# Shifts and scales of the norms as row sums on the vector engine

## The chip, the cores and the metric

One core of a Trainium2 chip runs the whole kernel. The metric is the device time of one execution in microseconds. Engines: PE is the matrix engine, PEld its weight loads, DVE the vector engine, ACT the scalar engine, POOL the general engine, SP the engine that issues most transfers.

## The reference

A two-layer decoder trunk on 256 tokens of width 1024, all in float32. Before every sub-layer stands a norm whose shift and scale come from one conditioning vector `c`:

```python
c_act = jax.nn.silu(c)
mod = jnp.einsum('bd,dn->bn', c_act, w_ada[layer]) + b_ada[layer]
sh1, sc1, gt1, sh2, sc2, gt2 = [m[:, None, :] for m in jnp.split(mod, 6, axis=-1)]
h = rms_norm(x, g_attn[layer]) * (1.0 + sc1) + sh1
x = x + gt1 * hybrid_mixer(h, ...)
h = rms_norm(x, g_ffn[layer]) * (1.0 + sc2) + sh2
x = x + gt2 * (swiglu(h, ...) if layer == 0 else moe_swiglu(h, ...))
```

`w_ada` is 1024 x 6144 for each layer: a vector times a matrix, of which each layer needs six pieces of 1024 columns (shift, scale and gate, twice). Layer 0 ends in a dense feed-forward of width 2816, layer 1 in a mixture of eight experts.

## The kernel before, in words

The kernel runs in the order: first norm, first attention, second norm, dense feed-forward, third norm, second attention, fourth norm, experts, last norm. Activations have tokens or features on the 128 partitions as needed; every large weight is loaded by SP into a ring of three `raw` buffers and split by ACT (line 164) and DVE (line 168) into two parts, which PE multiplies three times (lines 186 to 188, 340, 870 to 872).

The shift and scale of a norm are made by `Mod` (line 213), in two halves of 512 features. `half(q)` is a generator: it clears an accumulator `ada` on POOL and loads the bias row into it (lines 195, 197), then takes eight blocks of `w_ada`, 128 input features x 1024 columns (512 of the shift, 512 of the scale), each loaded by SP into one of two `rada` buffers (line 209) and added on DVE with `c` as the scalar of a partition (line 211). The sum over partitions is left to PE: eight products with a column of ones (line 233, sixteen PE instructions) put the 1024 sums into PSUM, 128 of them to a column, and DVE takes them from there (lines 239, 240). `gate` (line 245) makes a gate with the same accumulation and a product with a matrix of ones (line 255).

These generators are strewn into other work: `filler(parts, steps)` (line 921) gives a function `fill` that at its i-th call advances the generators by `steps[i]`; a step is two blocks, and each half or gate has five steps, the last being the sum and its reading. In attention `fill` is called at set places of the code (after the projections, after each branch and token half, and once with 20 to finish, line 794), in the feed-forward twice for each of its blocks and once with 30 before the last block (line 905). The first norm's halves are made by `Start` with the same accumulators, ahead of all else. Both halves of the second norm and a gate are made in the first attention (lines 938 to 940), a gate, the third norm, a gate and the fourth norm in the feed-forward (line 949), and one gate in the second attention (line 986).

A scheduler puts the traced instructions of each engine in an order of its own: an instruction whose inputs are free can move ahead of ones traced before it. In the two attentions, and in the feed-forward, `after_split` and `issue_after` hold some DVE work behind a given instruction. Every engine then works its list in order, so a waiting instruction holds what is behind it.

Of the kernel before, what the change touches and what calls it, by code (L numbers as in the profile page):

```python
# [12 lines left out]
F32 = mybir.dt.float32  # L13
# [35 lines left out]

RAW, RAWX, W1B, W2B, ADAB, RADA = 3, 6, 3, 3, 2, 2  # L50
PARTS = [2]
# [4 lines left out]
def trunk(ctx: ExitStack, tc: tile.TileContext, x, c, positions, w_in, w_out, diff_lambda, diff_subln,  # L56
# [10 lines left out]
    def ps_a(name):  # L67
        return psum.tile([P, 512], F32, tag="a", name=name, bufs=4)
# [14 lines left out]
    def pre1(shape, dt, name):  # L83
        return pre.tile(shape, dt, name=name, bufs=1)
# [6 lines left out]
    nc.gpsimd.dma_start(posi, positions.rearrange("b (t p) -> (b t) p", p=P))  # L91
    vrows = pre1([48, P], F32, "vrows")
    nc.gpsimd.dma_start(vrows[0:16], g_attn.rearrange("l (k p) -> (l k) p", p=P))
    nc.gpsimd.dma_start(vrows[16:32], g_ffn.rearrange("l (k p) -> (l k) p", p=P))
    nc.gpsimd.dma_start(vrows[32:48], b_ada[0, 0:2 * D].rearrange("(k p) -> k p", p=P))

# [116 lines left out]
    class Mod:  # L213


        def __init__(self, l, which, g0, queue):
            self.l, self.base, self.g0, self.queue = l, which * 3072, g0, queue
            self.piece = 3 * which
# [3 lines left out]
        def columns(self, q):  # L222
            return [self.base + 512 * q, self.base + D + 512 * q]
# [37 lines left out]
    gT = pre1([P, 4 * KC], F32, "gT")  # L261
    m1 = Mod(0, 0, 0, nc.scalar)

# [145 lines left out]
    with tc.tile_pool(name="start", bufs=1, reuse_waits="tile") as sp, tc.issue_after(silu_c.ins), in_order():  # L409

        bT = sp.tile([P, 2, KC], F32, name="bT")

        class Start:


            def __init__(self, q):
                self.q = q
                self.acc = pre.tile([P, 1024], F32, tag="ada", name="ada", bufs=ADAB)

            def sums(self):  # L420
                q = self.q
                pc = ps_b("pc")
                T.matmul(pc[:, 0:8].rearrange("p (a k) -> p a k", a=2), ident, bT[:, :, 4 * q:4 * q + 4],
                         start=True, stop=False)
# [13 lines left out]
        for k in range(KC):  # L438
            first.block(k)
            if k in (1, 5):  # L440
                t = k // 5
                nc.sync.dma_start(xs[:, t], x[0, t * P:(t + 1) * P, :])
                for n in range(2):
                    nm0.part(t, n)
                nm0.finish(t, True)
            if k == 5:
                pv = ps_c("pv")
                T.transpose(pv[:, 0:48], vrows, ident[:48, :48])
                V.tensor_copy(gT, pv[:, 0:32])
                V.tensor_copy(bT.rearrange("p a k -> p (a k)"), pv[:, 32:48])  # L450
        vi = pj_i.split(0, 4)
# [20 lines left out]
        pj_a.unit(0, 4, va, terms=(2,))  # L472
    ada_raw[:] = [pre, RADA]


# [461 lines left out]

    m2 = Mod(0, 1, 16, nc.gpsimd)
    finish = attention(0, h, pj_i, pj_a, filler([m2.half(0), m2.half(1), gate(0, 0, "g1")],
                                                 (0, 1, 0, 0, 4, 0, 0, 3, 1, 4, 1, 1)), yp)  # L940
    with tc.tile_pool(name="ffn", bufs=1, reuse_waits="tile") as fp:
# [3 lines left out]
        for t in range(NT):  # L945
            ffn.first(h, t, st["units"])
        m1 = Mod(1, 0, 8, nc.gpsimd)
        m2 = Mod(1, 1, 24, nc.gpsimd)
        fill = filler([gate(0, 1, "g2"), m1.half(0), m1.half(1), gate(1, 0, "g1"), m2.half(0), m2.half(1)], (3, 0, 1, 0, 3, 0, 6, 0, 6, 0, 0, 0, 0, 4, 2, 1, 1))
        nm = Norm("a1")  # L950
# [540 lines left out]
def _laid_out(name, a):  # L1491
# [7 lines left out]
    if name == "w_ada":  # L1499
        a = a.reshape(DEPTH, KC, P, 2, 3, 1024)  # L1500
        shift, scale = (a[..., i, :].reshape(DEPTH, KC, P, 2, 2, 512) for i in range(2))
        mods = np.stack([shift, scale], 5).reshape(DEPTH, KC, P, 2, 2, 1024)
        a = np.concatenate([mods, a[..., 2:, :]], 4).reshape(DEPTH, KC, P, 6, 1024)
        return a.transpose(0, 3, 1, 2, 4)
    if name in ("w_ff_gate", "w_ff_up"):
# [27 lines left out]
```

## Time and profile before

| | us |
|---|---|
| median of three runs | 1309.76 |
| lowest, highest | 1303.88, 1314.73 |
| the profiled execution | 1308.91 |
| its span, first to last instruction | 1307.1 |
| PE busy | 1230.5 (94%) |
| DVE busy | 1091.4 (83%) |
| ACT busy | 832.9 (64%) |

Busy times overlap, and a PE that shows as busy need not be at its peak: a row of its timeline gives start, length and, in brackets, the idle time in front of it with what ended it. [...] Rows of one timeline may overlap a little, because the next instruction starts while the one before it drains.

### The profile page before, as it was taken

Reading aid. Unit: us, or ns where it says so; the run is one execution under the profiler, and the core shown is the slowest. Engines: PE = TensorE matmul, PEld = TensorE weight load, DVE = VectorE, ACT = ScalarE, POOL = GpSimd, SP = SyncE. Lnnn points to the kernel's source line nnn. Section 1 sums busy time; section 2 is a strip of 40 time slices with the busy share of each in tenths; the row PEclk is TensorE's granted clock in tenths of the full one; section 3 lists DMA queues with packets and bytes.
Section 4 is the critical chain, followed back from the end, with each engine's and each line's share of the span. In section 5 each row is a group of like instructions: output and inputs, shape, how many; then the busy total and the mean of one; then the engine's idle time right before and its main releaser. Section 6 shows DMA issues by size and latency. Waiting matters only on the chain.

```text
span 1307.1 us, 17866 instructions
## 1 busy us (share of the span) xinstructions
PE 1230.5 (94%) x6601; PEld 1036.0 (79%) x6601; DVE 1091.4 (83%) x1236; ACT 832.9 (64%) x1010; POOL 52.5 (4%) x88
## 2 busy tenths in 40 slices
PE   4989899999999899899999999999999999999996
PEld 4779779989887787677888877788878778788784
DVE  7898677787768864687899987899986999978996
ACT  3654563433446555457788856788855898667785
POOL 3101000010001000000000000000000000000001
PEclk9999899999989899889999999999999999999999
DMA  9557828988963433568999998899998999998991
GB/s 382 206 170 239 293 93 309 318 315 302 331 241 113 137 122 129 225 235 290 385 396 420 419 412 308 324 404 420 421 382 292 358 419 420 420 350 319 410 361 56
DMA packets 63679, 396.90 MB, mean 304 GB/s; under 512 B 7718, under 2 KB 8032, under 8 KB 23264
## 3 DMA queue, kind: packets, MB, share of 16 engines
q1 hardware_dynamic: 62928, 395.60, 79.4%
q8 instruction: 54, 0.88, 0.3%
q14 instruction: 41, 0.34, 0.1%
q0 software_dynamic: 640, 0.07, 0.0%
q10 hardware_dynamic: 16, 0.00, 0.0%
HBM read 394.60 MB, written 1.05 MB: 303 GB/s over the span
## 4 chain that ended last, share of the span: by engine, by line
PE 62%; DVE 10%; issue 8%; ACT 4%; POOL 0%; POOLq 0%; ACTq 0%; DVEq 0%
DVE w L168 6%; PE gu L187 5%; PE gu L186 5%; PE gu L188 5%; PE gu L1269 4%; PE gu L1268 4%; PE dn L186 4%; PE dn L188 4%; PE dn L187 4%; PE pj L340 3%; PE dn L1268 3%; PE dn L1269 2%; PE ptl L1284 2%; PE gu L870 2%; PE gu L872 2%
## 5 line engine op out<-in xcount | busy, mean ns | idle before, releaser
L164 ACT ACTIVATE w<-raw 128x1024 fp32r<-128x1024 f32 (+3 forms) x203 | 258.9, 1293 | 164.4 <-PE gu L871 37.2
L168 DVE TENSOR_TENSOR w<-raw,w 128x1024 fp32r<-128x1024 f32 (+3 forms) x203 | 303.8, 1512 | 50.8 <-ACT w L164 50.3
L168 DVE TENSOR_TENSOR w<-rawx,w 128x2048 fp32r<-128x2048 f32 (+1 forms) x134 | 300.2, 2252 | 26.5 <-ACT w L164 26.2
L164 ACT ACTIVATE w<-rawx 128x2048 fp32r<-128x2048 f32 (+1 forms) x134 | 252.2, 1887 | 16.4 <-PE gu L187 9.2
L340 PE MATMUL pj<-w,h 128*128 128x384 f32 (+3 forms) x672 | 134.0, 351 | 1.2 <-ACT h L182 0.5
L211 DVE SCALAR_TENSOR_TENSOR ada<-rada,cT,ada 128x1024 f32<-128x1024 f32 x80 | 102.3, 1279 | 32.7 <-DMA rada<-in_w_ada 32.6
L340 PEld LDWEIGHTS pj<-w,h 128*128 128x128 f32 x672 | 112.9, 192 | 11.4 <-ACT h L182 2.4
L168 DVE TENSOR_TENSOR w2x<-rawx,w1x 128x2048 fp32r<-128x2048 f32 (+1 forms) x45 | 100.6, 2237 | 12.9 <-ACT w1x L164 12.9
L186 PE MATMUL gu<-w,hh 128*128 128x512 f32 (+1 forms) x288 | 110.5, 384 | 0.0
L1269 PE MATMUL gu<-w,hh 128*128 128x512 f32 (+1 forms) x288 | 107.4, 380 | 3.2 <-DVE w L168 2.8
L187 PE MATMUL gu<-w,hh 128*128 128x512 f32 (+1 forms) x288 | 109.2, 379 | 0.0
L188 PE MATMUL gu<-w,hh 128*128 128x512 f32 (+1 forms) x288 | 109.1, 379 | 0.0
L1268 PE MATMUL gu<-w,hh 128*128 128x512 f32 (+1 forms) x288 | 106.7, 377 | 0.0
L870 PE MATMUL gu<-h,w 128*128 128x256 f32 x320 | 91.5, 286 | 0.0
L872 PE MATMUL gu<-h,w 128*128 128x256 f32 x320 | 90.6, 283 | 0.0
L871 PE MATMUL gu<-h,w 128*128 128x256 f32 x320 | 90.5, 283 | 0.0
L164 ACT ACTIVATE w1x<-rawx 128x2048 fp32r<-128x2048 f32 (+1 forms) x45 | 84.4, 1878 | 4.7 <-PE gu L187 2.5
L1269 PEld LDWEIGHTS gu<-w,hh 128*128 128x128 f32 x288 | 54.1, 188 | 18.8 <-DVE w L168 8.5
L188 PEld LDWEIGHTS gu<-w,hh 128*128 128x128 f32 x288 | 54.6, 190 | 10.8
L187 PEld LDWEIGHTS gu<-w,hh 128*128 128x128 f32 x288 | 54.8, 190 | 10.4 <-issue 0.5
L186 PEld LDWEIGHTS gu<-w,hh 128*128 128x128 f32 x288 | 54.6, 190 | 10.5 <-issue 0.5
L1268 PEld LDWEIGHTS gu<-w,hh 128*128 128x128 f32 x288 | 54.1, 188 | 10.4
(348 smaller groups left out, 2508.7 us busy)
## 6 DMA issues: line engine op xcount, KB each, us to landing
rawx<-in_w_exp_down SPq DMA_DIRECT2D x72, 1024.0 KB, 7.4
rawx<-in_w_exp_up SPq DMA_DIRECT2D x55, 1024.0 KB, 7.6
rawx<-in_w_exp_gate SPq DMA_DIRECT2D x49, 1024.0 KB, 8.3
rada<-in_w_ada SPq DMA_DIRECT2D x96, 512.0 KB, 5.2
raw<-in_w_exp_gate SPq DMA_DIRECT2D x39, 1024.0 KB, 8.0
raw<-in_w_exp_up SPq DMA_DIRECT2D x33, 1024.0 KB, 7.8
raw<-in_w_exp_down SPq DMA_DIRECT2D x16, 1024.0 KB, 7.3
raw<-in_w_ff_gate SPq DMA_DIRECT2D x11, 1024.0 KB, 7.1
```

Source lines behind the costliest of these rows:

```text
L164: last_split[0] = A.activation(v1[:, s], r[:, s], AF.Copy)
L168: last_split[1] = V.tensor_tensor(v2[:, s], r[:, s], v1[:, s].bitcast(F32), op=ALU.subtract)
L186: T.matmul(ps, l1, r1, start=start, stop=False)
L187: T.matmul(ps, l2, r1, start=False, stop=False)
L188: T.matmul(ps, l1, r2, start=False, stop=stop)
L211: V.scalar_tensor_tensor(acc, r, cT[:, k:k + 1], acc, op0=ALU.mult, op1=ALU.add)
L340: T.matmul(o, (h1, h2, h1)[i][:, k, s], (v1, v1, v2)[i][:, j], start=(k == 0 and i == 0), stop=(k == KC - 1 and i == 2))
L870: T.matmul(pg[:, b], v1[:, k, s], h[0][:, k], start=(k == 0), stop=False)
L871: T.matmul(pg[:, b], v1[:, k, s], h[1][:, k], start=False, stop=False)
L872: T.matmul(pg[:, b], v2[:, k, s], h[0][:, k], start=False, stop=(k == KC - 1))
L1268: T.matmul(ps, l1, r1, start=start, stop=False)
L1269: T.matmul(ps, l1, r2, start=False, stop=stop)
```

## The change

The halves of all norms but the first are computed the other way round. `w_ada` is laid out on the host with output features on partitions and the 1024 input features along the row, `silu(c)` is held on all partitions as a row (`cB`), and each block of 128 outputs is one DVE instruction: product with `cB` and sum along the row, with the bias as the start value, written into one column of the shift or the scale. A half is again eight blocks of 512 KB and eight DVE instructions; no PE product, no clearing, no bias row and no PSUM bank. The biases come with four small loads into `vrows`, which is transposed at the start (96 rows in place of 48). The accumulator buffers go from two to one, since gates alone use them; the first norm's have a place of their own. The fourth norm's halves move from the feed-forward into the second attention, ahead of its gate, and the step lists are new.

```diff
-RAW, RAWX, W1B, W2B, ADAB, RADA = 3, 6, 3, 3, 2, 2
+RAW, RAWX, W1B, W2B, ADAB, RADA = 3, 6, 3, 3, 1, 2
-    vrows = pre1([48, P], F32, "vrows")
+    vrows = pre1([96, P], F32, "vrows")
...
-    nc.gpsimd.dma_start(vrows[32:48], b_ada[0, 0:2 * D].rearrange("(k p) -> k p", p=P))
+    for l in range(DEPTH):
+        for w in range(2):
+            nc.gpsimd.dma_start(vrows[32 * (l + 1) + 16 * w:32 * (l + 1) + 16 * w + 16],
+                                b_ada[l, w * 3072:w * 3072 + 2 * D].rearrange("(k p) -> k p", p=P))
     class Mod:
...
         def half(self, q):
-            cols = self.columns(q)
-            acc = ada_acc(self.l, cols, self.queue)
-            for k in range(0, KC, 2):
-                ada_step(acc, self.l, self.piece + q, (k, k + 1))
+
+            ks = slice(4 * q, 4 * q + 4)
+            for k in range(4 * q, 4 * q + 4):
+                for s in range(2):
+                    r = pre.tile([P, 1024], F32, tag="rada", name="rada", bufs=RADA)
+                    nc.sync.dma_start(r, w_ada[self.l, 3 * self.which + q, 2 * (k % 4) + s])
+                    with after_split(not early[0]):
+                        V.tensor_tensor_reduce(out=r, in0=r, in1=cB, scale=1.0,
+                                               scalar=bT[:, self.l, self.which, s, k:k + 1], op0=ALU.mult,
+                                               op1=ALU.add, accum_out=(self.sh, self.gain)[s][:, k:k + 1])
                 yield
-            pc = ps_a("pc")
-            for j in range(8):
-                T.matmul(pc[:, j:j + 1], acc[:, j * P:(j + 1) * P], ones[:, 0:1], start=True, stop=True)
-            self.take(q, pc)
+            V.scalar_tensor_tensor(self.gain[:, ks], self.gain[:, ks], 1.0, gT[:, self.g0 + ks.start:self.g0 + ks.stop],
+                                   op0=ALU.add, op1=ALU.mult)
             yield
...
-                self.acc = pre.tile([P, 1024], F32, tag="ada", name="ada", bufs=ADAB)
+                self.acc = sp.tile([P, 1024], F32, name=f"acc{q}")
...
+    cB = pre1([P, D], F32, "cB")
+    nc.scalar.dma_start(cB, bass.AP(tensor=c.tensor, offset=c.offset, ap=[[0, P], [1, D]]))
+    A.activation(cB, cB, AF.Silu)
...
-        fill = filler([gate(0, 1, "g2"), m1.half(0), m1.half(1), gate(1, 0, "g1"), m2.half(0), m2.half(1)], (3, 0, 1, 0, 3, 0, 6, 0, 6, 0, 0, 0, 0, 4, 2, 1, 1))
+        fill = filler([gate(0, 1, "g2"), m1.half(0), m1.half(1), gate(1, 0, "g1")], (3, 0, 1, 0, 3, 0, 4, 0, 4, 0, 0, 0, 0, 4, 1, 0, 0))
...
-    finish = attention(1, h, pj_i, pj_a, filler([gate(1, 1, "g2")], (0, 1, 0, 0, 0, 1, 1, 2)), yp)
+    finish = attention(1, h, pj_i, pj_a, filler([m2.half(0), m2.half(1), gate(1, 1, "g2")], (0, 1, 0, 0, 2, 1, 1, 2, 2, 2, 2, 2)), yp)
```

In the host's layout of `w_ada` only the first norm's pieces of layer 0 and the gates keep the old order.

## Rows read from the trace of the kernel before

**Rows 1.** Page, part 1: busy time, share of the span, instructions.

```profile
PE 1230.5 (94%) x6601; PEld 1036.0 (79%) x6601; DVE 1091.4 (83%) x1236; ACT 832.9 (64%) x1010; POOL 52.5 (4%) x88
```

**Rows 2.** Windows by stage: length, PE, PEld, DVE, ACT, POOL busy (count), clock, DMA share, GB/s.

```profile
0.00:46.00 46.00, 27.29 (x130) 23.77 (x131) 36.46 (x72) 19.39 (x38) 14.01 (x36) 1.00 0.87 341
46.00:172.00 126.00, 115.56 (x669) 99.46 (x669) 105.06 (x233) 71.77 (x176) 12.01 (x13) 0.96 0.64 219
192.00:358.00 166.00, 164.35 (x1173) 153.36 (x1172) 132.34 (x128) 64.47 (x76) 8.71 (x13) 1.00 0.89 312
401.00:527.00 126.00, 116.36 (x665) 99.35 (x664) 86.78 (x204) 70.56 (x174) 4.77 (x6) 0.97 0.38 130
566.00:1307.00 741.00, 717.81 (x3473) 583.00 (x3472) 659.90 (x453) 559.23 (x456) 4.35 (x4) 0.99 0.91 360
```

**Rows 3.** Groups by line and shape: count, busy us, mean ns, idle before.

```profile
L233 PE MATMUL pc<-ones,ada 128*128 128x1 f32 x96 | 11.6, 251 | 3.9 <-issue 3.9
L211 DVE SCALAR_TENSOR_TENSOR ada<-rada,cT,ada 128x1024 f32<-128x1024 f32 x80 | 102.3, 1279 | 32.7 <-DMA rada<-in_w_ada 32.6
```

**Rows 4.** Timeline of PE: the four column sums in the feed-forward (start, length, idle before).

```profile
259.91 1.84 PE L233 MATMUL pc<-ones,ada 128*128 128x1 f32 x16
...
280.04 1.92 PE L233 MATMUL pc<-ones,ada 128*128 128x1 f32 x16 [1.41 <-issue]
...
334.38 1.92 PE L233 MATMUL pc<-ones,ada 128*128 128x1 f32 x16 [0.24 <-issue]
...
360.86 2.28 PE L233 MATMUL pc<-ones,ada 128*128 128x1 f32 x16 [2.21 <-issue]
```

**Rows 5.** Timeline of DVE just before the last of them.

```profile
359.47 1.28 DVE L211 SCALAR_TENSOR_TENSOR ada<-rada,cT,ada 128x1024 f32<-128x1024 f32 x1 [0.60 <-DMA rada<-in_w_ada]
```

**Rows 6.** Windows of 4 us behind it, columns as in rows 2.

```profile
362.00:366.00 4.00, 4.00 (x21) 4.00 (x22) 3.73 (x6) 3.23 (x4) 0.00 (x0) 0.53 0.62 221
366.00:370.00 4.00, 4.00 (x24) 4.00 (x24) 2.81 (x3) 2.09 (x3) 0.00 (x0) 0.62 0.85 295
```

**Rows 7.** Timeline of the first attention: its two column sums, and what waits.

```profile
91.31 1.84 PE L233 MATMUL pc<-ones,ada 128*128 128x1 f32 x16
...
93.19 0.16 DVE L239 COPY sh<-pc 128x4 f32<-128x4 f32 x1 [1.27 <-PE pc L233]
...
120.22 1.84 PE L233 MATMUL pc<-ones,ada 128*128 128x1 f32 x16
...
121.29 1.58 ACT L164 ACTIVATE w<-raw 128x768 fp32r<-128x768 f32 x2 [5.18 <-DMA raw<-in_w_in]
```

**Rows 8.** Timeline: the same two instructions in the first and the second attention.

```profile
53.84 0.24 POOL L656 COPY qkA<-qkA 128x64 f32<-128x64 f32 x1 [3.63 <-ACT w L164]
...
171.96 0.69 DVE L815 TENSOR_TENSOR tmp<-wo,gt 128x512 f32<-128x512 f32 x1 [1.17 <-PE wo L188]
...
413.29 1.10 POOL L656 COPY qkA<-qkA 128x64 f32<-128x64 f32 x1 [5.23 <-DVE qkA L404]
...
527.55 0.69 DVE L815 TENSOR_TENSOR tmp<-wo,gt 128x512 f32<-128x512 f32 x1 [1.18 <-PE wo L188]
```

**Rows 9.** Groups and instructions by form: nearest rows to the new instruction.

```profile
L714 DVE SCALAR_TENSOR_TENSOR EB<-EB,rB 128x128 f32<-128x128 f32 x8 | 2.4, 347 | 0.1
...
L272 ACT ACTIVATION_READ_ACCUMULATOR xn<-xs x20: 185/186/202, 7.6 to 1298.1; 128x1 f32 x20
```

**Rows 10.** Timeline of the start: a bias load, the first transpose, the first block.

```profile
3.12 0.48 POOL L95 DMA_DIRECT2D vrows<-in_b_ada  x1
...
4.84 0.27 PE L107 MATMUL pcr<-ident,crow 8*128 8x8 f32 x1 [4.84 <-POOL ident masks.py:199]
...
8.77 0.74 DVE L433 TENSOR_SCALAR ada<-rada,cT 128x1024 f32<-128x1024 f32 x1
```

**Rows 11.** Windows of the first attention around its slow clock, columns as in rows 2.

```profile
132.00:136.00 4.00, 1.20 (x7) 0.67 (x6) 3.39 (x7) 0.70 (x2) 0.00 (x0) 1.00 0.93 329
136.00:147.00 11.00, 9.24 (x33) 7.55 (x34) 8.96 (x14) 7.44 (x20) 0.00 (x0) 0.54 0.90 307
```

More of the change, by code (lines that the diff above doesn't have):

```diff
@@ L213, in trunk, with __init__ @@
     class Mod:
-        def __init__(self, l, which, g0, queue):
-            self.l, self.base, self.g0, self.queue = l, which * 3072, g0, queue
-            self.piece = 3 * which
+        def __init__(self, l, which, g0):
+            self.l, self.which, self.g0 = l, which, g0
             self.sh = cst.tile([P, KC], F32, name=f"sh{l}{which}")
             self.gain = cst.tile([P, KC], F32, name=f"gain{l}{which}")
-        def columns(self, q):
-            return [self.base + 512 * q, self.base + D + 512 * q]
         def half(self, q):
-            cols = self.columns(q)
-            acc = ada_acc(self.l, cols, self.queue)
-            for k in range(0, KC, 2):
-                ada_step(acc, self.l, self.piece + q, (k, k + 1))
+            ks = slice(4 * q, 4 * q + 4)
[7 more added lines that the diff above has]
+                                               op1=ALU.add, accum_out=(self.sh, self.gain)[s][:, k:k + 1])
                 yield
-            pc = ps_a("pc")
-            for j in range(8):
-                T.matmul(pc[:, j:j + 1], acc[:, j * P:(j + 1) * P], ones[:, 0:1], start=True, stop=True)
-            self.take(q, pc)
+            V.scalar_tensor_tensor(self.gain[:, ks], self.gain[:, ks], 1.0, gT[:, self.g0 + ks.start:self.g0 + ks.stop],
+                                   op0=ALU.add, op1=ALU.mult)
             yield
@@ L261, in trunk @@
     gT = pre1([P, 4 * KC], F32, "gT")
-    m1 = Mod(0, 0, 0, nc.scalar)
+    bT = pre1([P, DEPTH, 2, 2, KC], F32, "bT")
+    m1 = Mod(0, 0, 0)
     class Norm:
@@ L409, in trunk @@
     with tc.tile_pool(name="start", bufs=1, reuse_waits="tile") as sp, tc.issue_after(silu_c.ins), in_order():
-        bT = sp.tile([P, 2, KC], F32, name="bT")
         class Start:
@@ L422, in sums @@
                 pc = ps_b("pc")
-                T.matmul(pc[:, 0:8].rearrange("p (a k) -> p a k", a=2), ident, bT[:, :, 4 * q:4 * q + 4],
+                T.matmul(pc[:, 0:8].rearrange("p (a k) -> p a k", a=2), ident, bT[:, 0, 0, :, 4 * q:4 * q + 4],
                          start=True, stop=False)
@@ L447, in trunk @@
                 pv = ps_c("pv")
-                T.transpose(pv[:, 0:48], vrows, ident[:48, :48])
+                T.transpose(pv[:, 0:96], vrows, ident[:96, :96])
                 V.tensor_copy(gT, pv[:, 0:32])
-                V.tensor_copy(bT.rearrange("p a k -> p (a k)"), pv[:, 32:48])
+                V.tensor_copy(bT.rearrange("p l w s k -> p (l w s k)"), pv[:, 32:96])
         vi = pj_i.split(0, 4)
@@ L936, in halves @@
         return each
-    m2 = Mod(0, 1, 16, nc.gpsimd)
+    m2 = Mod(0, 1, 16)
     finish = attention(0, h, pj_i, pj_a, filler([m2.half(0), m2.half(1), gate(0, 0, "g1")],
@@ L946, in trunk @@
             ffn.first(h, t, st["units"])
-        m1 = Mod(1, 0, 8, nc.gpsimd)
-        m2 = Mod(1, 1, 24, nc.gpsimd)
-        fill = filler([gate(0, 1, "g2"), m1.half(0), m1.half(1), gate(1, 0, "g1"), m2.half(0), m2.half(1)], (3, 0, 1, 0, 3, 0, 6, 0, 6, 0, 0, 0, 0, 4, 2, 1, 1))
+        m1 = Mod(1, 0, 8)
+        m2 = Mod(1, 1, 24)
+        fill = filler([gate(0, 1, "g2"), m1.half(0), m1.half(1), gate(1, 0, "g1")], (3, 0, 1, 0, 3, 0, 4, 0, 4, 0, 0, 0, 0, 4, 1, 0, 0))
         nm = Norm("a1")
@@ L1502, in _laid_out @@
         mods = np.stack([shift, scale], 5).reshape(DEPTH, KC, P, 2, 2, 1024)
-        a = np.concatenate([mods, a[..., 2:, :]], 4).reshape(DEPTH, KC, P, 6, 1024)
-        return a.transpose(0, 3, 1, 2, 4)
+        rows = np.concatenate([mods, a[..., 2:, :]], 4).reshape(DEPTH, KC, P, 6, 1024).transpose(0, 3, 1, 2, 4)
+        mods = a[..., :2, :].reshape(DEPTH, D, 2, 2, KC, P).transpose(0, 2, 4, 3, 5, 1).reshape(DEPTH, 2, 2, KC, P, D)
+        gates = rows.reshape(DEPTH, 2, 3, KC, P, D)[:, :, 2:]
+        a = np.concatenate([mods, gates], 2).reshape(DEPTH, 6, KC, P, D)
+        a[0, 0:2] = rows[0, 0:2]
+        return a
     if name in ("w_ff_gate", "w_ff_up"):
```

## The prediction

> **What bounds the kernel now.** I read the page first: PE is busy for 1230.5 us of the span of 1307.1, 94% [rows 1]. A mean over so much says little, so the windows by stage come next [rows 2]. In the feed-forward PE is busy for 164.35 of 166 us while DVE is busy for 132.34: there a PE instruction less is time less. In the two attentions PE shows 115.56 and 116.36 of 126 us, yet much of that is short chains PE, ACT, DVE and back; DVE has 21 us left in the first and 39 in the second, and the transfers take a share of 0.64 and 0.38. The last 741 us, the experts, hold no work of `w_ada` at all: the change can reach only what stands before them. Then I asked for the groups of the lines that go [rows 3]: the column sums of line 233 are 96 PE instructions, sixteen for each of six halves, with 3.9 us of idle time in front of them; the accumulating DVE instruction of line 211 takes 1279 ns. Last I looked at each column sum in its place in the timeline.
>
> **The column sums in the feed-forward.** All four halves made there lose theirs. Each sum stands in PE's list between two blocks of dense work, and PE cannot pass it. From the timeline [rows 4]: the first costs 1.84 us; the second 1.92, and 1.41 in which PE waited for the accumulation; the third 1.92 and 0.24. The fourth is the dear one: 2.28 us, and 2.21 us of waiting, because the call with 30 steps pushes the rest of the generators into one place, where DVE itself waits for a block of `w_ada` [rows 5]. [...] Together 1.84 + 3.33 + 2.16 + 4.49 + 2.9 = **14.7 us**. What could be late next: DVE's splits. With sixteen accumulations of 1.28 us moved away (20.5 us), DVE's 132 us fall to about 112, plus a little for the dearer new instruction, beside a PE stage of some 155, and SP has 8 MB less to bring. So I let the whole sum stand; its lower end is what remains if the gap of 2.21 and the slow clock stay for another reason, 9.6.
>
> **The new instruction.** It reads two float32 rows of 1024, as line 211 does, and writes a sum besides. The scalar-times-tensor form takes 347 ns for 128 columns [rows 9] and 1279 ns for 1024 [rows 3], so (1279 - 347) / 896 = 1.04 ns a column, with two float32 sources. I take the same for the new one. For writing out the sum no DVE row exists; the nearest is ACT's separate accumulator read, a record of 186 ns [rows 9] that overlaps its neighbour. From both ends: nothing, since a store of one column may hide in the drain, up to 0.19 us; nothing excludes a gain either, but none of the rows shows one. I take 0.1 us, 1.38 us in all.
> [...]
>
> **First attention.** It keeps its 24 blocks (two halves and a gate) and loses two column sums. The first stands in the chain of the softmax, and DVE waits 1.27 us for it, PE works 1.84 [rows 7]: I take 1.8. The second lies where ACT has just waited 5.18 us for projection weights [rows 7], so PE would soon wait for those instead: nothing, at best 1.84. The sixteen read-outs add 1.6 us to a DVE that is busy for 105 of 126 us; half of it on the path, 0.8. Net **-1.0**, between -3.7 and +2.2.
>
> **Second attention.** It receives sixteen row sums, 16 x 1.38 = 22 us of DVE, and 8 MB on SP's queue, in order among the projection weights; the next load waits behind a `rada` load that waits for its buffer, which waits for DVE. Ends: 0 and 22 us. The nearest row is the first attention, which is the same program with the sixteen. From the second copy of line 656 to the first gated product of line 815, so without the different beginnings, it takes 171.96 - 53.84 = 118.1 us; the second 527.55 - 413.29 = 114.3 [rows 8]. So sixteen more instructions, two column sums (3.7 us of PE) and their transfers cost 3.8 us between them. The new place has no column sums but dearer instructions, and they sit behind `after_split`, where DVE's next maximum or split is queued behind each and PE waits for that. I take **+4**.
>
> **What costs nothing.** At the start three more bias loads of 0.48 us on POOL put the first transpose from 4.84 to about 6.3, and the first block begins at 8.77 [rows 10] behind other DVE work: cover of 2.4 us; without it up to 1.4. The broadcast of `c` is 512 KB, 1.5 us at the 341 GB/s of the start [rows 2], and one ACT instruction on an engine busy for 19 of 46 us: 0, at most 1.5. Clearing and bias loads of the accumulators vanish from a POOL that nobody waits for there (12 of 126 us busy, 8.7 of 166). One accumulator buffer is enough, as only gates remain and each is summed before the next is begun. The closing multiplication of a half is the same small DVE instruction as before.
>
> **Sum.** -14.7 - 1.0 + 4 = -11.7 us. The profiled execution took 1308.9 (span 1307.1 and 1.8 around it) and would take 1297.2; the median of the three runs is 0.9 higher, so I predict **1298 us**, with 1292 to 1306 as this case's own range. About 1%, 13.1 us, is what a measurement of this kernel can tell from no change; the bound of "faster" is 1296.7, so the forecast lies just on the slow side of it.
>
> **Rivals.**
> *All of it hides* (chance 0.30). The second attention has 39 us of idle DVE and a transfer share of 0.38 [rows 2], so it takes the sixteen for nothing, and both column sums of the first attention count: 14.7 + 3.7 = 18.4 us, about 1291. Against it: the chains of the softmax have no slack for a DVE instruction of 1.4 us in the wrong place.
> *The second attention pays for it* (0.13). All sixteen lie bare on the path, and weights held up behind `rada` loads open a gap for PE. The first attention shows the pattern: PE busy for 1.20 of 4 us with transfers at 0.93, then 11 us at a mean clock of 0.54 [rows 11], 5 us lost. 22 + 5 = 27 against 15.7 gained: +11, about 1321, slower than before. It decides as soon as the stage pays more than 15.7. Against it: the first attention's total with the same load.
> *The new instruction runs at half rate* (0.06). If the sum along the row takes a second cycle for each column, it costs 1.04 x 1024 = 1.07 us more, 2.35 in all. Feed-forward: hidden, as DVE stays near 130 of 155. First attention: 16 x 1.07 = 17 us against 21 idle, half to all of it on the path. Second: 16 x 2.35 = 38 us against 39 idle, likewise 19 to 38. With -16.5 for the sums that go, +11 to +38, and about 1334 in the middle. For it speaks no row; against it the 1.04 ns of the older form.
> [...]
> *The gap at 358 us stays* (0.08). Without the column sum PE waits there for the splits of the next block instead, since ACT and DVE too were waiting for transfers [rows 5]. Then 9.6 in place of 14.7: about 1303.
>
> **How the numbers follow.** The forecast has 0.43, of which a third lies under 1296.7. Faster by over 1%: 0.30 + 0.13 = 0.43. Slower by over 1%, above 1322.9: the half rate 0.06 and the upper part of the paying stage 0.07, 0.13. The rest, 0.44, is within 1%. The range goes from 1286, the hidden case with a fast run, to 1321, where the paying stage is taken in to its middle and the half rate left out.
>
> **What would show it.** Line 233 gone, and PE in the feed-forward busy without breaks to its last block; that stage shorter by about 15 us, its clock at 1.00 behind the place of the old gap. The new DVE instruction at 1.28 to 1.47 us, 48 of them; at 2.3 the half rate is right. The first attention shorter by 1 to 4 us; the second longer by about 4 between the two marks, with sixteen row sums in it; a clock below 0.9 there, or ACT waiting on projection weights for more than a few us, speaks for the paying stage. The experts as long as before; if they differ by more than 3 us, something that I have not named moved, such as the order in which the scheduler lays the work, and the forecast is wrong for that reason.

## The result, and the profile after

The kernel after the change takes **1295.39 us** (median of six runs, 1292.02 to 1298.34) against 1310.88 for the kernel before (six runs, the three above among them, 1302.38 to 1314.73): ratio 0.9892, 95% interval 0.9861 to 0.9922; by the ratio that is 14 us less, between 10 and 18. Run again in a later session it gave 0.9884 (0.9842 to 0.9926). Ratios, here and below, are of fast runs, which leaves out one of ten executions of e2_rows_stay, at 6731 us. The profiled execution took 1295.81 us, its span 1294.1, against 1308.91 and 1307.1: 13.0 us less.

Page of after, part 1, then its windows by stage, cut at the matching places (columns as in [rows 2]; the clock is the mean that PE was granted, 1.00 its full speed):

```profile
PE 1216.9 (94%) x6505; PEld 1023.1 (79%) x6505; DVE 1090.3 (84%) x1278; ACT 833.4 (64%) x1011; POOL 42.3 (3%) x73
```

```profile
0.00:46.00 46.00, 26.05 (x127) 22.35 (x128) 36.02 (x71) 19.87 (x37) 12.98 (x35) 1.00 0.88 345
46.00:166.00 120.00, 110.80 (x639) 94.67 (x639) 106.27 (x247) 71.79 (x177) 6.54 (x8) 0.99 0.67 232
187.00:339.00 152.00, 152.00 (x1090) 142.20 (x1089) 113.88 (x124) 63.12 (x74) 2.94 (x4) 1.00 0.84 298
382.00:513.00 131.00, 118.93 (x669) 101.83 (x669) 104.53 (x238) 69.73 (x172) 6.60 (x5) 0.96 0.57 190
553.00:1294.00 741.00, 716.72 (x3470) 582.18 (x3469) 660.03 (x453) 559.20 (x456) 4.34 (x4) 0.99 0.91 360
```

The 96 column-sum products are gone from PE (6601 to 6505). In this window of the feed-forward PE is busy without a break, 152.00 of 152 us; the second attention's DVE went from 87 of 126 us [rows 2] to 105 of 131; the experts are as they were. DVE does about as much as before in the whole run. Its new instruction, in groups by line and shape, is to be set beside [rows 3]:

```profile
L232 DVE CUSTOM_DVE_ANT_0 rada<-rada,cB,bT 128x1024 f32<-128x1024 f32 x48 | 61.2, 1277 | 13.5 <-DMA rada<-in_w_ada 13.4
L214 DVE SCALAR_TENSOR_TENSOR ada<-rada,cT,ada 128x1024 f32<-128x1024 f32 x32 | 41.0, 1280 | 11.0 <-DMA rada<-in_w_ada 10.7 <-DVE kTC L751 0.3
...
L232 DVE DVE_READ_ACCUMULATOR2_ANT gain<- 128x1 f32 x24 | 2.0, 82 | 0.0
```

1277 ns for the row sum, and 82 ns for writing it out (the other 24 records write `sh`). Most of the 82 lies under the end of the row sum's own record, as in the timeline of DVE, where both end at 82.80:

```profile
81.52 1.28 DVE L232 CUSTOM_DVE_ANT_0 rada<-rada,cB,bT 128x1024 f32<-128x1024 f32 x1
82.72 0.08 DVE L232 DVE_READ_ACCUMULATOR2_ANT sh<- 128x1 f32 x1
```

For the division by stage I use four marks that both traces have: the copy of `qkA` and the first gated product `tmp` of an attention [rows 8], and the first gated product of the feed-forward (381.99 us before). In the timeline of after:

```profile
53.49 0.24 POOL L662 COPY qkA<-qkA 128x64 f32<-128x64 f32 x1 [3.63 <-ACT w L167]
...
166.31 0.69 DVE L821 TENSOR_TENSOR tmp<-wo,gt 128x512 f32<-128x512 f32 x1 [1.11 <-PE wo L191]
...
362.34 0.69 DVE L821 TENSOR_TENSOR tmp<-dn,gt 128x512 f32<-128x512 f32 x1 [0.39 <-PE dn L191]
...
394.97 1.10 POOL L662 COPY qkA<-qkA 128x64 f32<-128x64 f32 x1 [5.00 <-DVE qkA L409]
...
513.04 0.69 DVE L821 TENSOR_TENSOR tmp<-wo,gt 128x512 f32<-128x512 f32 x1 [1.14 <-PE wo L191]
```

| between the marks, us | before | after | difference | forecast |
|---|---|---|---|---|
| start, to the first mark | 53.84 | 53.49 | -0.35 | 0 |
| first attention | 118.12 | 112.82 | -5.30 | -1.0 |
| second norm and feed-forward | 210.03 | 196.03 | -14.00 | -14.7 |
| third norm, projections | 31.30 | 32.63 | +1.33 | 0 |
| second attention | 114.26 | 118.07 | +3.81 | +4 |
| fourth norm, experts, last norm | 779.55 | 781.06 | +1.51 | 0 |

The feed-forward between its marks, as one window of before and one of after:

```profile
171.96:381.99 210.03, 203.61 (x1418) 188.93 (x1417) 162.93 (x172) 87.88 (x114) 9.84 (x15) 0.98 0.80 287
```

```profile
166.31:362.34 196.03, 193.67 (x1352) 179.72 (x1351) 143.35 (x166) 88.03 (x114) 4.07 (x6) 0.99 0.74 264
```

PE's idle time in it falls from 6.42 to 2.36 us, by 4.06. Its busy time falls by 9.94, of which the four column sums are 7.96 by their rows [rows 4]. For the 1.98 that is left I know no other row than the clock behind the old gap, 0.53 and 0.62 before [rows 6] and 1.00 now, as the next windows show. Another profile of after (r0 below) has 3.56 of idle time and 194.76 busy, so each of these is good to about 1 us.

The place of the old gap, timeline of PE in after where the last block follows the tenth (before: the column sum at 360.86 with 2.21 us of waiting [rows 4]), and the windows just behind it (before: clock 0.53 and 0.62 [rows 6]):

```profile
346.05 0.39 PE L190 MATMUL dn<-w,gs 128*128 128x512 f32 x1
346.27 0.39 PE L191 MATMUL dn<-w,gs 128*128 128x512 f32 x1
346.50 0.28 PE L876 MATMUL gu<-h,w 128*128 128x256 f32 x1
```

```profile
347.00:351.00 4.00, 4.00 (x37) 4.00 (x36) 2.14 (x3) 1.38 (x2) 0.00 (x0) 1.00 0.95 332
351.00:355.00 4.00, 4.00 (x37) 4.00 (x36) 1.65 (x2) 1.87 (x3) 0.00 (x0) 1.00 0.80 334
```

### The profile page after: what moved, and what is told of

The parts are those of the page before. It is cut to its first block, busy times and chain, and to the rows that moved or that the text cites. A ratio compares the mean times of both kernels' runs of the same rounds, so it can differ in the third digit from the quotient of the medians.

```text
span 1294.1 us, 17663 instructions
## 1 busy us (share of the span) xinstructions
PE 1216.9 (94%) x6505; PEld 1023.1 (79%) x6505; DVE 1090.3 (84%) x1278; ACT 833.4 (64%) x1011; POOL 42.3 (3%) x73
## 4 chain that ended last, share of the span: by engine, by line
PE 69%; DVE 15%; ACT 6%; issue 5%; DMA 3%; POOL 1%; ACTq 0%; POOLq 0%; DVEq 0%; SPq 0%
DVE w L171 6%; PE gu L190 5%; PE gu L191 5%; PE gu L189 5%; PE gu L1275 4%; PE gu L1274 4%; PE dn L189 4%; PE dn L191 4%; PE dn L190 4%; PE pj L345 3%; PE gu L876 3%; PE gu L878 3%; PE gu L877 3%; PE dn L1274 3%; PE ptl L1290 3%
## 5 line engine op out<-in xcount | busy, mean ns | idle before, releaser
L876 PE MATMUL gu<-h,w 128*128 128x256 f32 x320 | 89.7, 280 | 0.0
L878 PE MATMUL gu<-h,w 128*128 128x256 f32 x320 | 89.4, 279 | 0.0
L877 PE MATMUL gu<-h,w 128*128 128x256 f32 x320 | 89.3, 279 | 0.0
L232 DVE CUSTOM_DVE_ANT_0 rada<-rada,cB,bT 128x1024 f32<-128x1024 f32 x48 | 61.2, 1277 | 13.5 <-DMA rada<-in_w_ada 13.4
L191 PEld LDWEIGHTS gu<-w,hh 128*128 128x128 f32 x288 | 54.7, 190 | 10.8
```

The lines of the kernel that those rows point to most:

```text
L191: T.matmul(ps, l1, r2, start=False, stop=stop)
L232: V.tensor_tensor_reduce(out=r, in0=r, in1=cB, scale=1.0, scalar=bT[:, self.l, self.which, s, k:k + 1], op0=ALU.mult, op1=ALU.add, accum_o ...
L876: T.matmul(pg[:, b], v1[:, k, s], h[0][:, k], start=(k == 0), stop=False)
L877: T.matmul(pg[:, b], v1[:, k, s], h[1][:, k], start=False, stop=False)
L878: T.matmul(pg[:, b], v2[:, k, s], h[0][:, k], start=False, stop=(k == KC - 1))
```

## The experiments

The theory to be tested is the forecast's: the feed-forward gives back the column sums on PE, each with its wait and the slow clock behind it. The rival: it gains because sixteen DVE instructions and 8 MB were moved out of it. The first two runs complete a square of which before and after are the other corners. All stage lengths are between the marks above, one profile each, and they scatter. The kernel after, profiled twice, differs from itself by 0.4 us in the attentions and by 2.3 in the feed-forward. The five profiles with its lists up to the end of the feed-forward (after, r0, b1, b2 and e6) lie between 112.8 and 114.4 in the first attention and between 194.9 and 198.3 in the feed-forward. The three that have the first attention of before (before, e1 and e4) lie between 117.0 and 118.1 there. Smaller differences than these, 1.6 us in an attention and 3.4 in the feed-forward, say nothing.

| | ratio to before (95%) | first attention | feed-forward | second attention |
|---|---|---|---|---|
| before | 1 | 118.1 | 210.0 | 114.3 |
| e1_move_only | 1.0029 (1.0002 to 1.0055) | 117.0 | 207.2 | 120.0 |
| e2_rows_stay | 0.9960 (0.9934 to 0.9985) | 113.0 | 206.8 | 114.0 |
| after | 0.9892 (0.9861 to 0.9922) | 112.8 | 196.0 | 118.1 |
| r0_after_again | 0.9884 (0.9842 to 0.9926) | 113.2 | 198.3 | 117.7 |
| e3_dead_sums | 1.0032 (1.0003 to 1.0060) | 116.8 | 206.8 | 120.8 |
| e4_spread | 1.0082 (1.0056 to 1.0107) | 117.0 | 219.3 | 113.7 |
| e5_stt_accum | 0.9896 (0.9857 to 0.9935) | 114.7 | 196.9 | 119.3 |
| e6_double | 1.0047 (1.0026 to 1.0068) | 114.2 | 194.9 | 138.6 |
| e7_rows_no_load | one execution | 117.0 | 197.4 | 114.9 |
| e8_half_back | 0.9957 (0.9934 to 0.9980) | 113.5 | 200.3 | 120.1 |
| e9_att_no_load | one execution | 118.1 | 195.7 | 119.5 |
| b1_early_list | 0.9929 (0.9889 to 0.9968) | 113.4 | 196.5 | 115.0 |
| b2_late_list | 0.9916 (0.9890 to 0.9942) | 114.4 | 194.9 | 117.5 |

**The move alone** (e1). In the kernel before, the two step lists of after:

```diff
-        fill = filler([gate(0, 1, "g2"), m1.half(0), m1.half(1), gate(1, 0, "g1"), m2.half(0), m2.half(1)], (3, 0, 1, 0, 3, 0, 6, 0, 6, 0, 0, 0, 0, 4, 2, 1, 1))
+        fill = filler([gate(0, 1, "g2"), m1.half(0), m1.half(1), gate(1, 0, "g1")], (3, 0, 1, 0, 3, 0, 4, 0, 4, 0, 0, 0, 0, 4, 1, 0, 0))
-    finish = attention(1, h, pj_i, pj_a, filler([gate(1, 1, "g2")], (0, 1, 0, 0, 0, 1, 1, 2)), yp)
+    finish = attention(1, h, pj_i, pj_a, filler([m2.half(0), m2.half(1), gate(1, 1, "g2")], (0, 1, 0, 0, 2, 1, 1, 2, 2, 2, 2, 2)), yp)
```

> The kernel before, column sums kept, with only the two halves of the fourth norm moved from the feed-forward into the second attention (both step lists as after the change). Theory (the column sums on TensorE are what the feed-forward gives back): two of its four go, the third and the fourth with the gap and the slow clock behind it, 2.16 + 4.49 + 2.9 = 9.6 us; the stage between the first gated product of the first attention and that of the feed-forward goes from 210.0 to about 200.5 us. The second attention takes the sixteen steps and two column sums, 114.3 to 118 to 122. Total 1303 to 1307 us. Rival (the feed-forward gains because VectorE and the transfers have less to do there): the stage is as short as after the change, 196 to 197, and the total 1299 to 1303.

Neither. The stage fell by 2.8 us only, no more than the scatter, although two of its four column sums were gone. What the remaining two cost is in PE's timeline and in the windows around the second of them:

```profile
258.41 1.84 PE L233 MATMUL pc<-ones,ada 128*128 128x1 f32 x16
...
281.92 3.55 PE L233 MATMUL pc<-ones,ada 128*128 128x1 f32 x16 [4.79 <-issue]
```

```profile
278.00:282.00 4.00, 0.08 (x1) 0.11 (x1) 3.80 (x4) 0.15 (x1) 0.00 (x0) 0.69 0.75 248
282.00:286.00 4.00, 4.00 (x18) 3.90 (x19) 2.05 (x5) 1.57 (x2) 0.47 (x1) 0.50 0.80 270
286.00:290.00 4.00, 4.00 (x12) 3.08 (x11) 4.00 (x5) 0.00 (x0) 1.44 (x3) 0.53 0.81 279
```

The first costs 1.84 as before; the second waits 4.79 where it waited 1.41 [rows 4], takes 3.55, and the granted clock is 0.50 and 0.53 in the windows from 282 to 290 us. The reason for the wait stands in DVE's timeline, which waits for a block of `w_ada`:

```profile
278.20 1.28 DVE L211 SCALAR_TENSOR_TENSOR ada<-rada,cT,ada 128x1024 f32<-128x1024 f32 x1 [2.93 <-DMA rada<-in_w_ada]
279.40 1.22 DVE L168 TENSOR_TENSOR w<-raw,w 128x1024 fp32r<-128x1024 f32 x1
280.54 1.28 DVE L211 SCALAR_TENSOR_TENSOR ada<-rada,cT,ada 128x1024 f32<-128x1024 f32 x1
```

**The row sums alone** (e2). The step lists of before put back into the kernel after.

> The kernel after the change, row sums kept, with the fourth norm's two halves left in the feed-forward (both step lists as in the kernel before). Theory (column sums): the feed-forward stays at 196 to 198 us although VectorE is given its sixteen instructions and 8 MB back; the second attention returns from 118.1 to about 114.3; total 1291 to 1294 us, below both kernels. Rival (relief of VectorE and the transfers in the feed-forward): the stage returns to 205 to 210, total 1301 to 1306.

The second attention returned to 114.0 as expected; the feed-forward did not stay at 196, it went to 206.8. There is no column sum in it, yet PE stands still for 5.30 us at the last block. PE's row, then ACT's rows in front of it:

```profile
369.03 0.79 PE L189 MATMUL dn<-w,gs 128*128 128x512 f32 x1 [5.30 <-ACT gs L185]
```

```profile
367.40 1.06 ACT L167 ACTIVATE w<-raw 128x1024 fp32r<-128x1024 f32 x1 [2.65 <-DMA raw<-in_w_in]
368.37 0.61 ACT L185 ACTIVATE gs<-g 128x512 fp32r<-128x512 f32 x1
```

The product `gs` that PE needs is queued on ACT behind the split of a projection weight that has not landed. So each part of the change by itself gives the stage some 3 us (2.8 and 3.2), which the scatter could be, and both together 14.0. Over the whole kernel, where the intervals do tell them apart, it is alike: +0.3% and -0.4% apart, -1.1% together.

**Is it the 8 MB or DVE?** (e7) As the run before, but the sixteen row sums of the fourth norm read a resident tile (`st["dry"]`, whose making at the start is not shown):

```diff
+                    dry = self.l == 1 and self.which == 1
+                    if dry:
+                        r = st["dry"]
+                    else:
-                    r = pre.tile([P, 1024], F32, tag="rada", name="rada", bufs=RADA)
-                    nc.sync.dma_start(r, w_ada[self.l, 3 * self.which + q, 2 * (k % 4) + s])
+                        r = pre.tile([P, 1024], F32, tag="rada", name="rada", bufs=RADA)
+                        nc.sync.dma_start(r, w_ada[self.l, 3 * self.which + q, 2 * (k % 4) + s])
```

> The earlier run with row sums and the fourth norm's halves left in the feed-forward, but the sixteen row sums of that norm work on one resident tile: their 8 MB are not loaded, VectorE's work is the same. The norm's values are then not those of the reference, so only the stages up to the second attention are to be read. Theory (the 5.3 us gap at the last block of that run is a transfer that comes late, all loads standing in one queue at a share of 0.9 to the end): without the 8 MB the stage is 196 to 198 us, as after the change. Rival (VectorE is too full there for its splits): 203 to 207.

197.4, as the theory said: what the stage could not take back were the loads, not DVE's instructions. Windows at the end of the stage, first of the run with the loads, then of this one, then of after:

```profile
318.00:342.00 24.00, 23.95 (x180) 22.79 (x180) 19.32 (x25) 10.00 (x12) 0.00 (x0) 1.00 0.93 338
342.00:366.00 24.00, 20.20 (x133) 17.75 (x131) 20.68 (x27) 12.29 (x15) 0.00 (x0) 1.00 0.87 324
366.00:374.00 8.00, 4.97 (x13) 3.92 (x14) 3.65 (x5) 2.53 (x3) 0.00 (x0) 0.57 0.93 370
```

```profile
318.00:342.00 24.00, 24.00 (x178) 22.56 (x177) 11.46 (x11) 10.61 (x13) 1.44 (x2) 1.00 0.70 258
342.00:366.00 24.00, 24.00 (x174) 22.61 (x173) 15.70 (x16) 13.99 (x18) 0.00 (x0) 1.00 0.70 250
```

```profile
318.00:342.00 24.00, 24.00 (x169) 21.88 (x168) 13.76 (x13) 12.39 (x16) 1.44 (x2) 1.00 0.50 168
342.00:366.00 24.00, 24.00 (x152) 21.45 (x151) 15.22 (x19) 10.99 (x17) 0.00 (x0) 1.00 0.71 254
```

Read the DMA share, the last column but one: 0.93, 0.87 and 0.93 with the loads, at most 0.71 without. This is one execution. It also takes 117.0 us in the first attention, where the kernels with row sums, no dead products and no resident tile take 112.8 to 114.7: the scheduler lays DVE's work in front of the mask in another order there. I take no reading from that stage of it.

**The PE block by itself** (e3). The kernel after, with at the end of each half eight products that nobody needs, called dead sums here:

```diff
+            pc = ps_a("pc")
+            for j in range(8):
+                T.matmul(pc[:, j:j + 1], r[:, j * P:(j + 1) * P], ones[:, 0:1], start=True, stop=True)
+            self.junk = pre1([P, 8], F32, f"junk{self.l}{self.which}{q}")
+            V.tensor_copy(self.junk, pc[:, 0:8])
```

> The kernel after the change with, at the end of each of its six halves, eight products of the old shape (128 x 128 weights, one column) on the last weight block, into PSUM, and a copy of the result into a tile that nobody reads: the old PE block put back, and nothing else of the old way (no accumulator, no bias load, no clearing). Theory: the feed-forward gets two of them back, 2 x 1.9 us and 0 to 1.4 of waiting for each, 196.0 to 200 to 203; the first attention 112.8 to 115 to 118; the second 118.1 to 120 to 122; total 1304 to 1311 us. Rival (the gain came from the bias loads, the clearing and the memory layout, or from the order in which the scheduler lays the work): 1294 to 1298 us.

The total, 1311.84 us, is above that of the kernel before, a little above the theory's range and far from the rival's: the block on PE, with the reading of its result by DVE, takes the gain away, and bias loads, clearing and layout are not needed for that. That a block more also changes the scheduler's order is not excluded. Two blocks in the feed-forward cost 10.8 us, where I expected 4 to 7. The second one's row, and the windows around it:

```profile
284.53 3.40 PE L238 MATMUL pc<-ones,rada 128*128 128x1 f32 x16 [3.75 <-DVE gain L232]
```

```profile
280.00:284.00 4.00, 0.78 (x4) 0.32 (x2) 3.33 (x5) 1.55 (x2) 0.00 (x0) 1.00 0.82 272
284.00:288.00 4.00, 3.47 (x17) 3.50 (x18) 1.02 (x4) 0.03 (x1) 0.00 (x0) 0.59 0.56 216
288.00:292.00 4.00, 4.00 (x11) 3.14 (x12) 3.67 (x5) 0.00 (x0) 0.00 (x0) 0.56 0.59 172
```

Again a wait for the stream of `w_ada` (3.75; DVE's last two blocks ahead of it waited 2.63 and 0.67 for their loads), a slow sum (3.40), and a granted clock of 0.59 and 0.56 in the windows from 284 to 292 us. The first attention is 4.0 us longer than in after, the second 2.7.

**Spreading the steps** (e4). One list in the kernel before, of which only the numbers are shown:

```diff
-(3, 0, 1, 0, 3, 0, 6, 0, 6, 0, 0, 0, 0, 4, 2, 1, 1)
+(3, 0, 1, 0, 3, 0, 3, 1, 3, 1, 3, 1, 3, 1, 3, 2, 2)
```

> The kernel before with one list changed: the 30 steps of the feed-forward's generators are spread over its calls (3,0,1,0,3,0,3,1,3,1,3,1,3,1,3,2,2), so that none are left for the call that takes up to 30 at once ahead of the last block. Theory as in the forecast (the fourth column sum is dear because of its place): its wait of 2.21 us and the slow clock behind it, 2.9, go; the stage 210.0 to about 205 us, total 1304 to 1306. Rival (PE waits there for a late transfer or split whatever the list): the gap stays or turns up elsewhere, the stage 209 to 211, total 1308 to 1312.

Slower than either theory allowed: the stage 219.3. The fourth sum lost its wait, as the theory said, but the third met a stream that was later still:

```profile
339.79 3.57 PE L233 MATMUL pc<-ones,ada 128*128 128x1 f32 x16 [7.93 <-DVE ada L211]
...
372.07 1.84 PE L233 MATMUL pc<-ones,ada 128*128 128x1 f32 x16
```

So the place of a sum does decide, but spreading the steps evenly moves the wait to another sum and does not remove it.

**Half of it back** (e8). Lists in after, without the start of their lines: one half of the fourth norm in the last blocks of the feed-forward, the other in the second attention.

```diff
-... gate(1, 0, "g1")], (3, 0, 1, 0, 3, 0, 4, 0, 4, 0, 0, 0, 0, 4, 1, 0, 0))
+... gate(1, 0, "g1"), m2.half(0)], (3, 0, 1, 0, 3, 0, 4, 0, 4, 0, 0, 0, 0, 4, 1, 2, 2))
-... filler([m2.half(0), m2.half(1), gate(1, 1, "g2")], (0, 1, 0, 0, 2, 1, 1, 2, 2, 2, 2, 2))
+... filler([m2.half(1), gate(1, 1, "g2")], (0, 1, 0, 0, 0, 1, 1, 1, 1, 2, 2, 1))
```

> The kernel after the change with one of the fourth norm's two halves (4 MB, eight row sums) back in the feed-forward, its steps put at the calls from 310 us on, where the transfers of the kernel after have a share of 0.40 to 0.60 between 318 and 342 us; the other half stays in the second attention. Theory (the feed-forward has room for about 4 MB there, and each VectorE instruction less in the second attention is worth about 0.24 us): feed-forward 196 to 198, second attention 118.1 to about 116, total 1292 to 1296 us. Rival (the transfers behind those steps, the weights of the last blocks and of the next projections, come late again): feed-forward 199 to 206, total 1298 to 1304.

The rival: 200.3, above all profiles with the lists of after, and 1302.61 in total, again with a wait at the last block that ends with `gs`, behind a projection weight that ACT waits for (1.91 us):

```profile
364.23 0.50 PE L189 MATMUL dn<-w,gs 128*128 128x512 f32 x1 [2.21 <-ACT gs L185]
```

The second attention took 120.1 with eight row sums, more than 118.1 with sixteen; so it does not pay by the piece.

**What the second attention pays for.** Two doses on the kernel after: a second row sum behind each of its sixteen on the same tile (e6: sixteen more on DVE, no load more; the line that makes the tile `extra` is not shown), and the resident tile in place of its loads (e9: DVE the same, 8 MB less; the edit as in e7, with the lists of after).

```diff
+                        if self.l == 1 and self.which == 1:
+                            V.tensor_tensor_reduce(out=r, in0=r, in1=cB, scale=1.0,
+                                                   scalar=bT[:, self.l, self.which, s, k:k + 1], op0=ALU.mult,
+                                                   op1=ALU.add, accum_out=self.extra[:, k:k + 1])
```

> The kernel after the change with each of the sixteen row sums of the second attention followed by a second one on the same tile, into columns that nobody reads: sixteen VectorE instructions more (22 us), no transfer more. Theory (the 3.8 us that the second attention pays are VectorE's instructions in front of its chains and splits): it pays about as much again or more, 118.1 to 121 to 128, total 1298 to 1305 us. Rival (it pays for the 8 MB in SP's queue, or for the order of the work): 117 to 119, total 1293 to 1297.

> The kernel after the change, but the sixteen row sums of the second attention work on one resident tile, so that their 8 MB are not loaded; VectorE's instructions and the list of steps are the same. The norm's values are not those of the reference, so only the stages up to the end of the second attention are to be read. Theory (the 3.8 us that the stage pays are VectorE's instructions, 1.28 us apiece, in front of its chains and splits): the second attention stays at 117 to 120 us. Rival (weights of the last projections come late behind the row blocks in SP's queue, transfers having a share of 0.84 to 0.93 there): back to 114 to 115.5.

138.6, far above the theory's 121 to 128, and 119.5. Sixteen more instructions cost 20.5 us. Taking away the loads gave nothing back; but that is one execution, and it takes 118.1 us in the first attention, so the scheduler's order differs in it as in e7, and it clears the loads of the 3.8 us only as far as that order does not matter. Windows of the stage between the marks, before, after, without loads, doubled:

```profile
413.00:527.00 114.00, 105.09 (x608) 89.98 (x607) 77.64 (x191) 62.11 (x158) 3.37 (x4) 0.97 0.36 123
```

```profile
395.00:513.00 118.00, 106.72 (x609) 91.63 (x608) 94.75 (x222) 61.74 (x158) 5.41 (x4) 0.96 0.58 191
```

```profile
399.00:519.00 120.00, 107.29 (x613) 91.88 (x612) 95.73 (x224) 61.57 (x158) 4.30 (x4) 0.97 0.35 126
```

```profile
395.00:534.00 139.00, 114.23 (x611) 96.67 (x610) 114.46 (x254) 62.05 (x158) 5.10 (x4) 0.90 0.49 168
```

From before to after DVE's busy time rises by 17 us and the stage by 4, so most of it found room. From after to doubled DVE's rises by another 20, and the stage by 20. That these are 1.28 us apiece is no sign that each lies bare at its full length: PE's idle time grows by 13.5 us (from 11.28 to 24.77), and the other 7.5 are the same PE instructions taking longer, at a mean clock of 0.90 in place of 0.96.

**The other form of the sum** (e5), with the bias added apart (the lines that add it are not shown):

```diff
-                        V.tensor_tensor_reduce(out=r, in0=r, in1=cB, scale=1.0,
...
+                        V.scalar_tensor_tensor(out=r, in0=r, scalar=1.0, in1=cB, op0=ALU.mult, op1=ALU.mult,
+                                               accum_out=(self.sh, self.gain)[s][:, k:k + 1])
```

> The kernel after the change with the row sum made by the other instruction of VectorE that can write an accumulator: scalar times tensor times tensor, (r x 1.0) x cB, with accum_out, the bias added by one small instruction for each of the two vectors of a half. [...] By the row of the kernel before for the same form without an accumulator (1279 ns) and the 1277 ns of the new instruction: 1.28 to 1.36 us, total 1294 to 1299.

```profile
L232 DVE SCALAR_TENSOR_TENSOR rada<-rada,cB 128x1024 f32<-128x1024 f32 x48 | 58.4, 1218 | 18.4 <-DMA rada<-in_w_ada 18.3
L232 DVE DVE_READ_ACCUMULATOR rada<-rada,cB 128x1 f32 x48 | 3.9, 81 | 0.0
```

1218 ns, and 0.9896 in total: the rival of half rate, at 2.35 us, falls for this form too. It is 59 ns shorter than the new instruction, which the time does not show.

**Other lists for the second attention** (b1, b2). Two lists for its fifteen steps, and the kernel after beside them (r0). Only the numbers of the first are shown; those of the second stand in what was expected of it.

```diff
-(0, 1, 0, 0, 2, 1, 1, 2, 2, 2, 2, 2)
+(0, 0, 0, 0, 4, 2, 2, 3, 1, 0, 0, 0, 1, 1)
```

> The kernel after the change, unchanged, on the same chip as the two lists beside it, so that they can be compared with it: 1292 to 1299 us, the second attention at 118 us, the other stages as in the first profile of it.

> The kernel after the change with another list for the fifteen steps of the second attention: (0,0,0,0,4,2,2,3,1,0,0,0,1,1) in place of (0,1,0,0,2,1,1,2,2,2,2,2), so that no step stands ahead of the mask and one instead of six among the three last projections; most stand among the softmax chains from 20 to 60 us of the stage, where row sums cost nothing by the marks of the kernel after. Theory (the stage pays by place: 1.7 us in front of the mask, 4.6 among the projections, where transfers have a share of 0.84 to 0.93 and VectorE is busy for 27 of 30 us): the second attention 114 to 116, total 1291 to 1295 us. Rival (sixteen VectorE instructions in the chains cost what they cost wherever they stand, as the doubled run's 1.28 us each): 118 to 124, total 1294 to 1302.

> As the list beside it, but (0,0,0,0,2,2,2,3,0,0,0,3,2,1): nothing among the three last projections, and six of the fifteen steps behind them, where VectorE in the kernel before is busy for 10 of 25 us and the transfers have a share of 0.06 to 0.25. Theory: the second attention 113.5 to 115.5, total 1290 to 1294 us, below the kernel after. Rival (the late loads hold up the weights of the output projection in SP's queue, or the sums the last norm, which needs them): 117 to 122, total 1294 to 1300.

The kernel after came out as said, 1295.32 and 117.7. The window of the stage with the early list:

```profile
396.00:511.00 115.00, 102.03 (x605) 87.30 (x604) 94.98 (x224) 60.71 (x156) 4.40 (x4) 1.00 0.57 196
```

It takes 115.0 in this profile, as the theory said, with the same sixteen row sums and the same 8 MB. What it gains is the clock, and not less waiting: PE is idle for 12.97 us in it against 11.28 in after, but its work takes 102.03 us at 1.00 in place of 106.72 at 0.96. Its median, 1298.44, is in the rival's range and not below the kernel after at 1295.32, and the intervals of the two overlap. The late list has 117.5 and 1297.39, both in the rival's range. Neither beats the kernel after in a way that these runs can show.

## Why the prediction was right

Forecast 1298, measured 1295.4; the likeliest case held, with a total of -13.0 in the profile against -11.7. Whether the kernel is faster by over 1%, to which I gave 0.43, or within 1%, 0.44, the runs leave open: the ratio is 0.9892, and its interval, 0.9861 to 0.9922, lies on both sides of 0.99. That the totals lie so close is in part luck. The first attention gave 4.3 us more than forecast; two stretches that I had put at nothing took 2.8 the other way, and the feed-forward gave 0.7 less.

*The feed-forward* came out at -14.0 against -14.7, with the clock behind the place of the old gap at 1.00, as said. Its three terms came out too, in this pair of profiles: -4.06 of idle time where the forecast had 3.86 of waits, the sums 7.96, and 1.98 for the clock where it had 2.9. No run shows the 2.9 by itself: the two windows behind the old gap have 0.53 and 0.62 [rows 6], 0.47 x 4 + 0.38 x 4 = 3.4 us of full speed, of which I left out 0.5 as lying under the sum, an estimate; what the two profiles show in its place is the 1.98. As a sum this was right, and as prices of single sums it was not: by it, the third and fourth sum with the gap were worth 9.6 us, but the run in which just these two went, with their blocks of `w_ada`, gained 2.8. The cost of a column sum is not its own. PE joins the stream of `w_ada` there and waits for however late that stream is: nothing to 2.21 us in the kernel before, 4.79, 3.75 and 7.93 in three variants. Behind those of 0.24 and 1.41 us in the kernel before, the granted clock is 1.00 in the next 4 us; behind 2.21 it is 0.53 and 0.62 in two windows [rows 6], behind 4.79 0.50 and 0.53, behind 3.75 0.59 and 0.56; behind 7.93 the sum itself takes 3.57 us. Remove some of the sums, or move their steps, and another takes the wait. The reason that I gave for the fourth, the call with 30 steps, is right for its own wait, which went with the call in e4, but not for the stage, which got longer there.

*What would be late next.* I let the whole sum stand because SP has 8 MB less to bring; that sentence carried more than it said. With row sums and the 8 MB left in place, the rival "the gap stays" came true in another form, 5.30 us behind a late projection weight, and the 14.0 shrank to 3.2. DVE, which I named first, was not what came next (197.4 without the loads). The rival's remark that ACT too was waiting for transfers has no line in [rows 5], which is DVE's alone; the trace of before bears it out, with ACT idle for 3.63 us until 361.92 for a load of `w_ff_down`.

*First attention*, the mis-sized term: -5.3 where I had -1.0 and -3.7 as the end. The term left out the clock. Behind the same wait for the C branch, the windows of 11 us show 0.54 before [rows 11] and in after:

```profile
133.00:144.00 11.00, 9.73 (x46) 8.42 (x47) 9.97 (x15) 7.88 (x20) 0.00 (x0) 0.84 0.93 309
```

That is 0.46 x 11 = 5.1 us lost before and 0.16 x 11 = 1.8 after, 3.3 us of the 5.3. Why the slow stretch is shorter was not tested; PE's wait in front of it is 1.85 before and 2.09 after, so not by that wait. How much of the 5.3 is due to PE's sums is not shown. The dead sums put 4.0 back, but with a slow stretch in another place: behind the C branch that run has 1.00, and earlier 0.59, where after has 1.00. The run with the resident tile (e7), which has no sum on PE, shows the same stretch and takes 117.0. The window of that place with the dead sums (with the resident tile its clock is 0.57):

```profile
93.88:101.88 8.00, 6.87 (x25) 5.26 (x24) 6.35 (x18) 4.08 (x18) 0.00 (x0) 0.59 0.59 157
```

So a term of a few us in an attention moves by as much when the scheduler lays the work differently.

*Second attention*: +3.8 for +4. The size held; the reason given, DVE instructions in front of chains, is not fully shown. The stage does not pay by the piece: eight row sums cost 5.8 us more than before, sixteen 3.8, and the same sixteen in other places 0.7. The transfers alone are not the reason either, as far as e9 tells. What changes with the place is in part the clock, 0.96 in after and 1.00 in b1, which the +4 did not have. That a load waits for its `rada` buffer until DVE gives it back shows in after: SP's queue waits for a row sum six times there, 22.1 us in all. The upper end of 22 us, all sixteen bare, is near what the next sixteen cost (20.5), but 7.5 us of that, over a third, were PE's instructions taking longer, at a clock of 0.90. The rival "all of it hides" fell with the 3.8 us; "the second attention pays for it" fell because 17 us more of DVE's busy time made the stage only 3.8 us longer.

*The new instruction*: 1277 ns and 82 for the accumulator, forecast 1.28 and 0.1. The trace shows two records for each. The rival of half rate fell for both forms: the trace of e5 has 1218 ns for the scalar-tensor-tensor form with an accumulator, that of before 1279 without. The rival's 2.35 us leaves out the 0.1 for the accumulator that the forecast has, and the upper end of +2.2 in the first attention has no working; neither bears on the outcome.

*Not foreseen*: +1.3 in the third norm's stretch and +1.5 behind the second attention. The first stays open: against before it is -0.4 with the row sums alone and +1.3 with the move alone, but also +1.0 in e7, where the row sums stayed in place and only the 8 MB were left out of the feed-forward, and +2.8 with the list spread. The second differs by up to 4.8 us (779.1 to 783.9) between profiles of kernels that have the same work there, and is no finding.

## What to carry to other kernels

In this kernel a reduction that ended on the matrix engine made that engine wait for the stream behind the reduction, up to 2.21 us before and 7.93 in e4; ended on the engine that consumes the stream, it let PE go on, busy for 152.00 of 152 us in after. Price such a wait by how late the stream can be and by the clock behind it, not by the instruction. And a change with two parts is not the sum of its parts: in the feed-forward each alone was worth a quarter of both or less, because removing PE's wait only helped where the transfers could keep up. Last, give a stage's length its scatter before reading it: with one profile each, 3 us of 200 could be nothing.

## What the runs showed of the hardware

The form with two float32 sources and an accumulator ran at the rate of the form without, 1218 (e5) to 1277 ns (after) for 1024 columns against 1279 (before), and the accumulator was written by a record of its own, 81 to 82 ns, most of it under the end of the sum's record. Behind the waits of PE of 3.75 (e3), 4.79 (e1) and 5.30 us (e2) in the feed-forward the windows show a granted clock of 0.50 to 0.59. Counted from where PE works again until the clock is back at 1.00, the mean is 0.60 over 8.47 us (284.53:293.00), 0.57 over 9.08 (281.92:291.00) and 0.63 over 5.97 (369.03:375.00). That is 3.4, 3.9 and 2.2 us of full speed lost on top of each wait. A part of it is the length of the column sum itself, 3.40 and 3.55 us where it takes 1.84 at a clock of 1.00 (before, 259.91:261.75).
